# The state space mixer of a two-block model as thirty kinds of step in one fixed order on every engine, without tensor work on GpSimd

## The chip, the cores and the metric

One core of one Trainium2 chip runs the whole program as a single launch. The time is device microseconds (us) of that core. The kernel before took 2540.38 us in the median of three runs (2539.35 to 2540.84); the one execution that the profiler recorded took 2535.84 us.

Engines: PE (TensorE, the matrix engine; PEld is its weight load), DVE (VectorE), ACT (ScalarE), POOL (GpSimd), SP (SyncE, which issues the DMAs here). PE writes its results into PSUM, eight banks of 128x512 float32; DVE and ACT read them from there.

## The reference, cut to what matters

Two blocks of two layers each follow one another on x of 512 positions by 1024 features. Only the first mixer of the first block, a state space mixer, is touched by the change; it stands first in the program.

```python
def s5_mixer(x, a_re, a_im, log_dt, b_re, b_im, c_re, c_im, d_skip, w_glu, w_out):
    u = x.astype(f32).reshape(bsz, seq, SSM_GROUPS, SSM_GROUP)      # 64 groups of 16 features
    dt = jnp.exp(log_dt.astype(f32))[:, None]
    lam_re = jnp.minimum(a_re.astype(f32), -1e-4)
    mag = jnp.exp(lam_re * dt)
    lbar_re = mag * jnp.cos(lam_im * dt)                            # lam_im = a_im
    lbar_im = mag * jnp.sin(lam_im * dt)
...
    bb_re, bb_im = _cmul(coef_re[..., None], coef_im[..., None], b_re, b_im)
    bu_re = jnp.einsum('blgh,gph->lbgp', u, bb_re)
    bu_im = jnp.einsum('blgh,gph->lbgp', u, bb_im)
    _, _, s_re, s_im = lax.associative_scan(                        # s[t] = lbar * s[t-1] + bu[t]
        _ssm_combine, (a_seq_re, a_seq_im, bu_re, bu_im), axis=0)
    y = (jnp.einsum('lbgp,ghp->blgh', s_re, c_re) - jnp.einsum('lbgp,ghp->blgh', s_im, c_im))
    y = y.reshape(bsz, seq, D_MODEL) + d_skip * x
    h = jax.nn.gelu(y).astype(x.dtype)
    val, gate = jnp.split(h @ w_glu, 2, axis=-1)
    z = val * jax.nn.sigmoid(gate)
    return (z @ w_out).astype(x.dtype)
```

After it come a layer norm, a gated feed-forward layer, stick-breaking attention and its feed-forward layer, and then a second block of the same size with other mixers.

## The kernel before, in words

The 64 groups are worked off as eight octets of eight groups. Time is cut into 64 chunks of eight positions, so a group's input is a 128x64 tile (eight positions by sixteen features, by chunks) and an octet's tile is 128x512.

Before the octets, `ssm_params` computes the discretised coefficients for all groups on 128x64 tiles, on DVE, with two sines on ACT (L523, L524), and `ssm_powers` their powers, first for octets 0 and 1 (part 0), later for the others (part 1). An octet then goes through these stages:

- tables (`ssm_tables`, tiles `scr`, `xl`, `xh`): phases on DVE (L605, L609), sine and cosine on ACT;
- matrices (`ssm_mats`): outer products of powers with B and C, 128x1024 each (L625): `m1` and `m2`, summed into `m1` (L634), and `n1` and `n2`, summed into `n1` on POOL (L637). PE multiplies the eight 128x128 blocks of `m1` by `ic` (identity beside C, L648); ACT copies the result out as `bt` and as the `c7` columns (L649, L650); the skip term is added to `c7` on DVE (L655), and after two octets eight DMAs lay `c7` out as the block-triangular `toep`;
- states (`ssm_states`): PE multiplies `bt` by the input (L689); ACT swaps the halves of the result (`sx`), DVE and POOL rotate it by the tables (L701 to L703), DVE scans over chunks with the decay `rho` (L712, a TENSOR_TENSOR_SCAN), rotates it back, and writes `tst` (L714 to L718);
- output (`ssm_out`): PE adds `toep` times input (L733) and `tst` times `n1` (L736), ACT copies to `yo` (L738), PE transposes (L744), ACT applies the GELU (L748), and the result is split into a high part `xh` (ACT, L181) and a low part `xl` (DVE or, for three octets, POOL, L182).

The string `SSM_STEPS` lists the calls of these functions (T, A, B, C). Within what the list gives, a scheduler that works when the program is built orders each engine's instructions. Four blocks of the next layer (`glu`) are used as filling: their weights are loaded and split early (W; `wh` on ACT L174, `wl` on POOL L177), and each finished octet adds its twelve products to four PSUM banks `mm` (G; L196 to L198). The other four banks, `aux`, serve everything else in the mixer. The rest of `glu` follows with banks `acc` and `mm`.

POOL's share is set by `LO_GPSIMD`, `M2_GPSIMD`, `N2_VECTOR` and `DECAY_SCALAR`: by octet, which engine makes `xl`, `m2`, `n2` and the decay row.

Of the kernel before, what the change touches and what calls it, by code (L numbers as in the profile page):

```python
# [39 lines left out]
    "T3 P1 A0 T0 T7 A1 T1 T5 T4 B0 T2 B1 A2 A3 W0 B2 C0 A4 B3 C1 A5 C2 B4 A6 T6 G0 G1 C3 B5 A7 B6 C4 "  # L40
    "G2 B7 G3 C5 C6 C7 G4 G5 G6 G7"
)

LO_GPSIMD, M2_GPSIMD, N2_VECTOR, DECAY_SCALAR = (2, 6, 7), (1,), (0, 1, 3, 5, 6, 7), (0, 2)
# [23 lines left out]

class Kern:
    def __init__(self, tc, ins, out, ctx):  # L70
        self.tc, self.nc, self.i, self.out = tc, tc.nc, ins, out
        self.g = ctx.enter_context(tc.tile_pool(name="glob", bufs=1))
        self.n = 0
        self.ctx = ctx
        self.ph = None
        self.lo_pool = False
        self.nw = 0
        self.nb = 0
        self.boundary = ()
        self.consts()  # L80


    def nm(self, s):
        self.n += 1
        return f"{s}_{self.n}"
# [24 lines left out]
    def scr(self, dt=F32):  # L110
        return self.gt("scr", [P, T], dt, bufs=7)
# [353 lines left out]
    def vexp(self, x, sp):  # L465
# [17 lines left out]
        nc.vector.tensor_add(e, em1, two)  # L483
        t1 = sp()
# [4 lines left out]
    def ssm_params(self):  # L489
# [13 lines left out]
        dt, _ = self.vexp(ldt, sp)  # L503
# [10 lines left out]
        ki, kf, r = sp(I32), sp(), sp()  # L514
# [45 lines left out]
        m2 = sp()  # L560
        V.tensor_mul(m2, mag, mag)
        V.tensor_mul(m2, m2, m2)
        V.tensor_mul(self.rho, m2, m2)

    def ssm_powers(self, part):
# [7 lines left out]
        self.nc.gpsimd.memset(pr[:, 0], 1.0)  # L573
        self.nc.gpsimd.memset(pi[:, 0], 0.0)
# [25 lines left out]
    def ssm_tables(self, o):  # L600

        nc = self.nc
        ph = self.scr()
        v3 = lambda t: t.rearrange("p (g c) -> p g c", c=64)
        nc.vector.tensor_tensor(v3(ph), self.v8[:, 8 * o:8 * o + 8, None].to_broadcast([P, 8, 64]),  # L605
                                self.iota[:, None, :].to_broadcast([P, 8, 64]), op=ALU.mult)
        ki = self.scr()
        nc.scalar.activation(ki, ph, AF.Copy, bias=ROUND)
        nc.vector.scalar_tensor_tensor(ph, ki, ROUND, ph, op0=ALU.subtract, op1=ALU.subtract)  # L609
        s, c = self.gt("xl", [P, T], bufs=NM), self.gt("xh", [P, T], bufs=NM)  # L610
        nc.scalar.activation(s, ph, AF.Sin, scale=TWO_PI)
        nc.scalar.activation(c, ph, AF.Abs)
        nc.scalar.activation(c, c, AF.Sin, scale=-TWO_PI, bias=self.hpi)
        return c, s

    def ssm_mats(self, o, toep, half):
        nc = self.nc
        V = nc.vector
        G8 = slice(8 * o, 8 * o + 8)
        u, bc = self.inp[o]  # L620
        b1, b2, c1, c2 = (bc[:, k * P:(k + 1) * P].rearrange("p (g h) -> p g h", h=16) for k in range(4))

        def outer(eng, tag, bufs, tab, vec):
# [32 lines left out]
        return u, bt, n1  # L656

    def ssm_octet(self, o):

        nc = self.nc  # L660
        if o % 2 == 0:
            self.c7 = self.pt("c7", [P, 2 * P], bufs=2)
        self.half[o] = self.ssm_mats(o, self.c7, o % 2)
        if o % 2 == 0:
            return
        tp = self.toep[o // 2 % len(self.toep)]
        for j in range(8):
            n = 16 * (j + 1)
            nc.sync.dma_start(tp[0:n].rearrange("p (g m) -> p g m", g=16)[:, :, 16 * j:16 * j + 16],
                              self.c7[P - n:P].rearrange("p (g h) -> p g h", g=16))  # L670
        for k in (0, 1):
            self.mats[o - 1 + k] = (tp[:, k * 1024:(k + 1) * 1024], *self.half[o - 1 + k])
# [7 lines left out]
    def ssm_states(self, o):  # L680

        nc = self.nc
        V = nc.vector
        G8 = slice(8 * o, 8 * o + 8)
        tp, u, bt, n1 = self.mats[o]
        co, sn = self.tab[o]
        w = self.aux()
        for g in range(8):
            nc.tensor.matmul(w[:, 64 * g:64 * g + 64], bt[:, g * P:(g + 1) * P], u[:, 64 * g:64 * g + 64],  # L689
                             start=True, stop=True)  # L690

        def swapped(src):

            t = self.pt("sx", bufs=4)
            nc.scalar.activation(t[0:64], src[64:128], AF.Copy)
            nc.scalar.activation(t[64:128], src[0:64], AF.Copy)
            return t

        b = swapped(w)
        a = self.pt("sx", bufs=4)  # L700
        V.tensor_mul(a, co, w)  # L701
        nc.gpsimd.tensor_mul(b, sn, b)
        V.tensor_sub(a, a, b)  # L703
        dec = self.scr()
        d3 = dec.rearrange("p (g c) -> p g c", c=64)
# [47 lines left out]
    def ssm(self):  # L753
# [7 lines left out]
        with ssm_psum as self.ps, self.phase("ssm") as self.ph:  # L761
# [8 lines left out]
            for t in self.toep:  # L770
                nc.gpsimd.memset(t, 0.0)
# [890 lines left out]
```

## Time and profile before

| | |
|---|---|
| median of three runs | 2540.38 us |
| the profiled execution | 2535.84 us |
| its span, first to last instruction | 2534.1 us |
| PE, busy share of the span | 95% |
| DVE | 59% |
| ACT | 39% |
| POOL | 9% |
| last `mm` filling product starts, first `acc` product starts | 181.64, 181.87 us |

The mixer's octets lie in the first 182 us of the span; the program after that is a long run of matrix products. The shares of the table are means over all of it, so the start has to be read from a window of its own. A row of the timeline gives the start, the duration, the engine and line, the operation, output and inputs, shapes, the count of equal instructions in a row, and in brackets the idle time of the engine before it with what ended it. The start of the next row less the start of this one is the pitch at which an engine that doesn't wait works; the duration holds some overlap with the next. One matrix product of float32 operands stands in the trace as two instructions (128 of L648 for 64 in the program).

### The profile page before, as it was taken

The page shows a single profiled execution, that of the slowest core. Times are in us where ns is not written, and L with a number is a line of the kernel's source. Part 1 is how long each engine was busy: PE and PEld are TensorE (multiplying, and loading weights), DVE is VectorE, ACT ScalarE, POOL GpSimd, SP SyncE. Part 2 cuts the span into 40 slices and gives each one's busy share as a digit, 9 for nine tenths or more (in the row PEclk, how much of TensorE's full clock was granted, in tenths as well). Part 3 has the DMA queues.
Part 4 walks back from the last instruction along what each step waited for, and adds up shares of the span by engine and source line. Part 5 has one row for each costly group of instructions (what it writes and reads, how often), then busy time and mean ns, then how long its engine had stood idle before and what let it go on. Part 6 is the DMA issues. An engine that isn't in the chain of part 4 may idle for free. (4 is left out here: it accounts for less than half of the span.)

```text
span 2534.1 us, 30680 instructions
## 1 busy us (share of the span) xinstructions
PE 2404.2 (95%) x12040; PEld 1991.0 (79%) x12044; DVE 1482.7 (59%) x2495; ACT 995.3 (39%) x1541; POOL 219.8 (9%) x158
## 2 busy tenths in 40 slices
PE   1599999999999999999998899999999999999999
PEld 1578888888977778888886678888888887888888
DVE  9963743333677885333458787665435667665622
ACT  2563342222465644222235444333324554333321
POOL 6630100000100010000013201000000000200000
PEclk9799999999999999999999999999999999999999
DMA  3333122233221122222332112222332221223232
GB/s 103 49 62 112 67 100 100 93 93 100 65 92 59 51 67 84 100 100 89 98 97 74 52 42 76 99 92 100 94 98 66 86 84 67 85 99 100 91 111 74
DMA packets 99360, 213.36 MB, mean 84 GB/s; under 512 B 44544, under 2 KB 45184, under 8 KB 99216
## 3 DMA queue, kind: packets, MB, share of 16 engines
q1 hardware_dynamic: 99216, 211.40, 26.3%
q8 instruction: 95, 1.56, 0.3%
q14 instruction: 49, 0.40, 0.0%
HBM read 206.92 MB, written 2.10 MB: 82 GB/s over the span
## 5 line engine op out<-in xcount | busy, mean ns | idle before, releaser
L174 ACT ACTIVATE wh<-wr 128x1024 fp32r<-128x1024 f32 (+1 forms) x389 | 404.5, 1041 | 1011.0 <-PE mm L197 393.1
L177 DVE TENSOR_TENSOR wl<-wr,wh 128x1024 fp32r<-128x1024 f32 (+1 forms) x341 | 408.8, 1199 | 459.5 <-ACT wh L174 458.2
L197 PE MATMUL mm<-xl,wh 128*128 128x512 f32 (+1 forms) x1176 | 453.1, 386 | 0.9 <-DVE xl L182 0.8
L196 PE MATMUL mm<-xh,wh 128*128 128x512 f32 (+1 forms) x1176 | 451.3, 387 | 1.5 <-ACT xh L181 1.3
L198 PE MATMUL mm<-xh,wl 128*128 128x512 f32 (+1 forms) x1176 | 451.7, 385 | 0.0
L197 PE MATMUL acc<-xl,wh 128*128 128x512 f32 (+1 forms) x888 | 336.4, 379 | 6.8 <-DVE xl L182 6.8
L196 PE MATMUL acc<-xh,wh 128*128 128x512 f32 (+1 forms) x888 | 337.2, 380 | 1.2 <-ACT xh L181 1.0
L198 PE MATMUL acc<-xh,wl 128*128 128x512 f32 (+1 forms) x888 | 336.1, 379 | 0.0
L177 POOL TENSOR_TENSOR wl<-wr,wh 128x1024 fp32r<-128x1024 f32 (+1 forms) x48 | 114.6, 2389 | 1890.6 <-ACT wh L174 1825.0
L196 PEld LDWEIGHTS mm<-xh,wh 128*128 128x128 f32 x1176 | 222.4, 190 | 46.0 <-issue 2.9
L197 PEld LDWEIGHTS mm<-xl,wh 128*128 128x128 f32 x1176 | 223.3, 190 | 44.2 <-DVE xl L182 1.7
L198 PEld LDWEIGHTS mm<-xh,wl 128*128 128x128 f32 x1176 | 223.3, 190 | 41.9 <-issue 0.7
L197 PEld LDWEIGHTS acc<-xl,wh 128*128 128x128 f32 x888 | 167.3, 189 | 38.8 <-DVE xl L182 8.1
L196 PEld LDWEIGHTS acc<-xh,wh 128*128 128x128 f32 x888 | 167.5, 189 | 32.9 <-ACT xh L181 1.4
L198 PEld LDWEIGHTS acc<-xh,wl 128*128 128x128 f32 x888 | 167.6, 189 | 30.8
L196 PE MATMUL acc<-hh,wh 128*128 128x512 f32 (+1 forms) x396 | 145.1, 366 | 1.0 <-DVE v L294 1.0
L196 PE MATMUL mm<-hh,wh 128*128 128x512 f32 (+1 forms) x396 | 145.0, 366 | 0.5 <-DVE v L294 0.5
L197 PE MATMUL acc<-hl,wh 128*128 128x512 f32 (+1 forms) x396 | 145.2, 367 | 0.0
L197 PE MATMUL mm<-hl,wh 128*128 128x512 f32 (+1 forms) x396 | 144.8, 366 | 0.0
L198 PE MATMUL mm<-hh,wl 128*128 128x512 f32 (+1 forms) x396 | 144.7, 365 | 0.0
L198 PE MATMUL acc<-hh,wl 128*128 128x512 f32 (+1 forms) x396 | 144.7, 365 | 0.0
L648 PE MATMUL aux<-ic,m 128*128 128x144 f32 x128 | 30.6, 422 | 66.6 <-DVE m L634 62.0
(469 smaller groups left out, 3774.2 us busy)
## 6 DMA issues: line engine op xcount, KB each, us to landing
wr<-down_dram SPq DMA_DIRECT2D x64, 448.0 KB, 3.3
wr<-gu_g_dram SPq DMA_DIRECT2D x44, 512.0 KB, 3.2
wr<-gu_u_dram SPq DMA_DIRECT2D x44, 512.0 KB, 3.2
wr<-gate_dram SPq DMA_DIRECT2D x44, 512.0 KB, 3.2
wr<-up_dram SPq DMA_DIRECT2D x44, 512.0 KB, 3.2
wr<-down_dram SPq DMA_DIRECT2D x32, 512.0 KB, 3.5
wr<-sb_qkv_dram SPq DMA_DIRECT2D x24, 512.0 KB, 3.2
wr<-glu_dram SPq DMA_DIRECT2D x16, 512.0 KB, 3.3
```

Of the source, the lines that this page charges most:

```text
L174: nc.scalar.activation(hi[:, :cols], raw[:, :cols], AF.Copy)
L177: (nc.gpsimd if pool else nc.vector).tensor_sub(lo[:, :cols], raw[:, :cols], hi[:, :cols])
L196: nc.tensor.matmul(ps[:, c0:c1], wh[:, s], xh[k][:, c0:c1], start=st, stop=False)
L197: nc.tensor.matmul(ps[:, c0:c1], wh[:, s], xl[k][:, c0:c1], start=False, stop=False)
L198: nc.tensor.matmul(ps[:, c0:c1], wl[:, s], xh[k][:, c0:c1], start=False, stop=en)
L648: nc.tensor.matmul(p3[:, g - g0], m1[:, g * P:(g + 1) * P], ic[:, g], start=True, stop=True)
```

## The change

Each octet is written as thirty kinds of step (`octet`), and `SSM_STEPS` lists every step of every octet: a letter and the octet's number. The class `InOrder` ties each instruction on DVE, ACT and PE to the one issued before it on that engine, so all three keep the order of the list. The letters: a, b, c, d tables; m, q the outer products `m1`, `m2`; n, N the outer products `n1`, `n2`; i the C columns of `ic`; A, K the matrix products and their copies, in three parts; e, E the skip term and the eight DMAs; B, s, x, y, D, z, t, r, u the states; C, v, X, g, h, l the output and its split; P, Z the powers of part 1 and the phases; W, w, G the filling.

What differs in the work:

- `m1` and `m2` are no longer summed on DVE: PE multiplies both and adds in PSUM. The same holds for `n1` and `n2`, formerly summed on POOL.
- POOL has no tensor work left in the mixer; one 128x8 MEMSET for each octet stays. All sixteen `n1` and `n2`, all `m2`, all first rotations, all `xl` and the filling's `wl` are on DVE; all decay rows, the identity part of `ic` and the clearing of `toep1` are on ACT; the clearing of `toep0` is on DVE.
- The skip term comes laid out from memory (`dd`, 32x1024 instead of 16x64), so POOL's product and its tile go; rows 0 to 63 of the same tile `yd` take the place of `yo`.
- `scr` has nine buffers (seven), `bc` four (two), `n1` and `n2` two each, `tst` four (three).
- The phases and the last two squarings of `rho` move from `ssm_params` to the step Z; an unused part of the first exponential goes.

The diff, cut to its core:

```diff
 SSM_STEPS = (
-    "T3 P1 A0 T0 T7 A1 T1 T5 T4 B0 T2 B1 A2 A3 W0 B2 C0 A4 B3 C1 A5 C2 B4 A6 T6 G0 G1 C3 B5 A7 B6 C4 "
+    "q1 i0 i1 W2 q0 W3 m0 P0 A0 m1 K0 A0 P1 A1 K0 Z0 A0 K1 P2 D1 A1 D0 a1 D2 P3 i2 A1 K1 b1 n0 K1 i3 B1 D3 c1 K0 "
...
-LO_GPSIMD, M2_GPSIMD, N2_VECTOR, DECAY_SCALAR = (2, 6, 7), (1,), (0, 1, 3, 5, 6, 7), (0, 2)
...
+            def call(*args, **kw):
+                self.last = self.kern.after(f(*args, **kw), self.last)
+                for tag in self.kern.fresh:
+                    self.kern.after(self.last, self.kern.taken.get(tag))
+                    self.kern.taken[tag] = self.last
...
-        return self.gt("scr", [P, T], dt, bufs=7)
+        return self.gt("scr", [P, T], dt, bufs=9)
...
-        V.tensor_add(m1, m1, m2)
-        n1 = outer(nc.gpsimd, "n1", 4, pr[:, 1:9], c1)
-        n2 = outer(V if o in N2_VECTOR else nc.gpsimd, "n2", 1, pi[:, 1:9], c2)
-        nc.gpsimd.tensor_add(n1, n1, n2)
...
+                for g in range(g0, g0 + n):
+                    PE.matmul(p3[:, g - g0], L["m1"][:, g * P:(g + 1) * P], ic[:, g], start=True, stop=False)
+                    PE.matmul(p3[:, g - g0], L["m2"][:, g * P:(g + 1) * P], ic[:, g], start=False, stop=True)
...
-        dd = self.pt("dd", [P, P], bufs=1)[96:P]
-        nc.gpsimd.tensor_tensor(gs3(dd, 16), self.dr[96:P, G8, None].to_broadcast([32, 8, 16]),
-                                self.ident[96:P, None, 112:P].to_broadcast([32, 8, 16]), op=ALU.mult)
-        V.tensor_add(toep[96:P, h], toep[96:P, h], dd)
+        def e():
+            V.tensor_add(L["c7"][96:P, half], L["c7"][96:P, half], self.yd[96:P, o * P:(o + 1) * P])
...
-        nc.gpsimd.tensor_mul(b, sn, b)
-        V.tensor_sub(a, a, b)
+        def y():
+            V.tensor_mul(L["b"], L["sn"], L["b"])
+            V.tensor_sub(L["a"], L["a"], L["b"])
...
-        if o in DECAY_SCALAR:
-            nc.scalar.activation(d3, self.rho[:, G8, None].to_broadcast([P, 8, 64]), AF.Copy)
-        else:
-            nc.gpsimd.tensor_copy(d3, self.rho[:, G8, None].to_broadcast([P, 8, 64]))
-        nc.gpsimd.memset(d3[:, :, 0:1], 0.0)
+        def D():
+            L["dec"] = self.scr()
+            A.activation(gc(L["dec"]), self.rho[:, G8, None].to_broadcast([P, 8, 64]), AF.Copy)
+            nc.gpsimd.memset(gc(L["dec"])[:, :, 0:1], 0.0)
...
+                for hf, g in gg:
+                    PE.matmul(yk[hf], L["ts"][:, g, 0:64], L["n1"][:, g * P:(g + 1) * P], start=False, stop=False)
+                for hf, g in gg:
+                    PE.matmul(yk[hf], L["ts"][:, g, 0:64], L["n2"][:, g * P:(g + 1) * P], start=False, stop=True)
...
-        self.split(h, self.xh[o], self.xl[o], nc.gpsimd if o in LO_GPSIMD else nc.vector)
+        def l():
+            self.xl[o] = self.gt("xl", [P, T], F32R, bufs=8)
+            V.tensor_sub(self.xl[o], L["h_"], self.xh[o])
...
-            for t in self.toep:
-                nc.gpsimd.memset(t, 0.0)
-            self.tst = [self.pt(f"tst{k}", [P, 8, 65]) for k in range(3)]
+            nc.vector.memset(self.toep[0], 0.0)
+            nc.scalar.activation(self.toep[1].rearrange("p (n c) -> p n c", c=P),
+                                 self.ident[:, None, :].to_broadcast([P, 16, P]), AF.Copy, scale=0.0)
+            self.tst = [self.pt(f"tst{k}", [P, 8, 65]) for k in range(4)]
...
-                nc.gpsimd.tensor_copy(t[:, :, :P], self.ident[:, None, :].to_broadcast([P, 8, P]))
+                nc.scalar.activation(t[:, :, :P], self.ident[:, None, :].to_broadcast([P, 8, P]), AF.Copy)
...
+                    elif f == "w":
+                        w, raw = fill[o]
+                        self.nc.vector.tensor_sub(w[1], raw, w[0])
```

In the changed kernel every instruction of an octet bears the line of `InOrder`'s call, L84. Three places of the engines' orders follow; the words after the line are the operation, output, inputs and the shape of the output, with x3 for three equal ones.

POOL at the start of the octets, before: the filling's `wl`, the skip product `dd`, the outer products and their sums, a rotation (`sx`).

```order
L177 TENSOR_TENSOR wl_163_597<-wr_161_594,wh_162_596 128x1024
L653 TENSOR_TENSOR dd_96_364<-dr_11_94,ident_1_58 32x128
L177 TENSOR_TENSOR wl_166_603<-wr_164_600,wh_165_602 128x1024
L625 TENSOR_TENSOR n1_90_340<-pw00_18_103,bc_66_259 128x1024
L625 TENSOR_TENSOR n1_107_392<-pw00_18_103,bc_68_263 128x1024
L177 TENSOR_TENSOR wl_169_609<-wr_167_606,wh_168_608 128x1024
L177 TENSOR_TENSOR wl_172_615<-wr_170_612,wh_171_614 128x1024
L625 TENSOR_TENSOR m2_106_389<-pw30_21_106,bc_68_263 128x1024
L637 TENSOR_TENSOR n1_90_340<-n1_90_340,n2_91_342 128x1024
L625 TENSOR_TENSOR n1_145_527<-pw016_22_107,bc_70_267 128x1024
...
L702 TENSOR_TENSOR sx_127_466<-xl_99_372,sx_127_466 128x512
L710 MEMSET scr_129_473 128x8
```

The same engine now, from the clearing of `tst` to the first work after the mixer.

```order
L877 MEMSET tst0_6_84 128x8
L877 MEMSET tst1_7_85 128x8
...
L890 MEMSET pw00_20_104 128x16
...
L775 MEMSET scr_99_370 128x8
L775 MEMSET scr_101_380 128x8
...
L775 MEMSET scr_179_716 128x8
L187 MEMSET mean1_298_1434 128x128
L189 MEMSET ones_299_1436 128x128
L210 TENSOR_TENSOR wl_481_2455<-wr_479_2452,wh_480_2454 128x1024
```

All 1024- and 512-wide tensor work is gone from POOL between the two clearings; what it did stands on DVE, ACT or PE.

ACT at the start, before: the table load, the C columns of `ic`, the two sines of `ssm_params` (`sp`), a filling weight.

```order
L641 ACT_TABLE_LOAD
L641 ACTIVATE ic0_9_90<-bc_66_259 128x8x16
L641 ACTIVATE ic1_10_91<-bc_68_263 128x8x16
L523 ACT_TABLE_LOAD
L523 ACTIVATE sp25_51_186<-sp24_50_179 128x64
L524 ACTIVATE sp26_52_187<-sp24_50_179 128x64
L174 ACTIVATE wh_162_596<-wr_161_594 128x1024
L608 ACTIVATE scr_82_296<-scr_81_294 128x512
```

The same place now.

```order
L84 ACT_TABLE_LOAD
L84 ACTIVATE ic0_10_92<-bc_62_247 128x8x16
L84 ACTIVATE ic1_11_93<-bc_64_252 128x8x16
L873 ACTIVATE toep1_5_81<-ident_1_58 128x2048
L880 ACTIVATE ic0_10_92<-ident_1_58 128x8x128
L880 ACTIVATE ic1_11_93<-ident_1_58 128x8x128
L558 ACT_TABLE_LOAD
L558 ACTIVATE sp23_51_187<-rr_15_99 128x64
L559 ACTIVATE sp24_52_188<-rr_15_99 128x64
...
L84 ACTIVATE bt_91_321<-aux_88_311 128x384
```

The clearing of `toep1` and the identity part of both `ic` stand ahead of the two sines, which read `rr` and whose results `ssm_params` needs.

PE at the start of the octets, before: the matrix products of octets 0 and 1 and the first products with the input.

```order
L648 MATMUL aux_93_347<-ic0_9_90,m1_88_335 128x144 x3
L648 MATMUL aux_94_353<-ic0_9_90,m1_88_335 128x144 x3
L648 MATMUL aux_95_359<-ic0_9_90,m1_88_335 128x144 x2
L648 MATMUL aux_110_399<-ic1_10_91,m1_105_387 128x144 x3
L648 MATMUL aux_111_405<-ic1_10_91,m1_105_387 128x144 x3
L648 MATMUL aux_112_411<-ic1_10_91,m1_105_387 128x144 x2
L689 MATMUL aux_126_457<-v_65_258,bt_92_345 128x64 x8
L689 MATMUL aux_136_494<-v_67_262,bt_109_397 128x64 x8
```

The same place now.

```order
L84 MATMUL aux_88_311<-ic0_10_92,m1_85_299 128x144
L84 MATMUL aux_88_311<-ic0_10_92,m2_81_292 128x144
...
L84 MATMUL aux_92_324<-ic0_10_92,m1_85_299 128x144
L84 MATMUL aux_92_324<-ic0_10_92,m2_81_292 128x144
...
L84 MATMUL aux_93_337<-ic1_11_93,m1_89_318 128x144
L84 MATMUL aux_93_337<-ic1_11_93,m2_77_283 128x144
...
L84 MATMUL aux_97_356<-ic0_10_92,m1_85_299 128x144
L84 MATMUL aux_97_356<-ic0_10_92,m2_81_292 128x144
...
L84 MATMUL aux_104_395<-ic1_11_93,m2_77_283 128x144
L84 MATMUL aux_107_409<-v_63_251,bt_98_361 128x64 x8
L84 MATMUL aux_112_433<-v_61_246,bt_91_321 128x64 x8
```

Each block has two products, one with `m1` and one with `m2`; the parts of octets 0 and 1 are interleaved. Behind the mixer the engines' orders are those of before.

## Rows read from the trace of the kernel before

**Rows 1.** Stretches: length, busy us (instructions) of PE, PEld, DVE, ACT, POOL; clock; DMA
```profile
20.00:60.00 40.00, 7.18 (x28) 6.89 (x29) 39.94 (x72) 12.97 (x25) 25.87 (x10) 1.00 0.16 53
73.00:76.40 3.40, 3.22 (x12) 2.90 (x12) 3.40 (x5) 3.33 (x7) 0.32 (x1) 0.50 0.73 75
60.00:120.00 60.00, 34.26 (x217) 30.70 (x216) 59.75 (x46) 31.51 (x68) 40.03 (x24) 0.73 0.29 47
120.00:160.00 40.00, 36.10 (x260) 31.34 (x260) 35.43 (x35) 25.50 (x46) 23.95 (x18) 0.84 0.27 36
160.00:181.80 21.80, 20.79 (x172) 15.84 (x172) 9.45 (x14) 15.43 (x22) 4.57 (x5) 1.00 0.30 62
```

**Rows 2.** Timeline of PE: start, duration, operation, count
```profile
41.70 4.18 PE L648 MATMUL aux<-ic,m 128*128 128x144 f32 x16 [41.70 <-DVE m L634]
...
73.16 3.22 PE L648 MATMUL aux<-ic,m 128*128 128x144 f32 x12 [7.21 <-DVE m L634]
...
158.40 2.00 PE L689 MATMUL aux<-v,bt 128*128 128x64 f32 x16
...
165.18 0.71 PE L744 MATMUL aux<-ident,yo 64*128 64x64 f32 x8 [0.20 <-ACT yo L738]
...
166.09 0.39 PE L736 MATMUL aux<-n,tst 128*64 128x128 f32 x4
166.31 0.39 PE L733 MATMUL aux<-toep,v 128*64 128x128 f32 x4
...
181.64 0.39 PE L198 MATMUL mm<-xh,wl 128*128 128x512 f32 x1
181.87 0.39 PE L196 MATMUL acc<-xh,wh 128*128 128x512 f32 x1
```

**Rows 3.** Timeline of DVE
```profile
18.31 0.22 DVE L539 TENSOR_TENSOR lb<-sp,sp 128x64 f32<-128x64 f32 x1
18.44 0.22 DVE L540 TENSOR_TENSOR lb<-sp,sp 128x64 f32<-128x64 f32 x1
...
40.34 1.21 DVE L634 TENSOR_TENSOR m<-m,m 128x1024 f32<-128x1024 f32 x1
41.48 0.34 DVE L584 TENSOR_TENSOR pw<-scr,scr 128x192 f32<-128x192 f32 x1
...
44.29 0.68 DVE L605 TENSOR_TENSOR scr<-v,cst 128x512 f32<-128x512 f32 x1
44.89 0.54 DVE L582 TENSOR_TENSOR scr<-pw,coef 128x384 f32<-128x384 f32 x1
...
58.51 3.36 DVE L625 TENSOR_TENSOR m<-pw,bc 128x1024 f32<-128x1024 f32 x1
...
84.05 1.22 DVE L712 TENSOR_TENSOR_SCAN scr<-scr,sx 128x512 f32<-128x512 f32 x1
85.19 0.83 DVE L605 TENSOR_TENSOR scr<-v,cst 128x512 f32<-128x512 f32 x1
...
170.43 0.69 DVE L718 TENSOR_TENSOR tst<-scr,sx 128x512 f32<-128x512 f32 x1
```

**Rows 4.** Timeline of POOL
```profile
58.13 2.66 POOL L637 TENSOR_TENSOR n<-n,n 128x1024 f32<-128x1024 f32 x1 [3.43 <-DVE n L625]
60.87 2.88 POOL L625 TENSOR_TENSOR n<-pw,bc 128x1024 f32<-128x1024 f32 x1
```

**Rows 5.** DVE grouped by line and shape, 0 to 182 us: busy, mean ns
```profile
L625 DVE TENSOR_TENSOR m<-pw,bc 128x1024 f32<-128x1024 f32 x15 | 27.4, 1835 | 0.0
```

**Rows 6.** Timeline of ACT
```profile
8.04 0.31 ACT L641 ACTIVATE ic<-bc 128x128 f32<-128x128 f32 x1 [2.28 <-DMA bc<-bc_dram]
...
13.73 0.26 ACT L523 ACTIVATE sp<-sp 128x64 f32<-128x64 f32 x1 [4.08 <-DVE sp L521]
...
14.04 1.04 ACT L174 ACTIVATE wh<-wr 128x1024 fp32r<-128x1024 f32 x1
...
143.41 1.28 ACT L611 ACT_TABLE_LOAD   x1
```

More of the change, by code (lines that the diff above doesn't have):

```diff
@@ L75, in __init__ @@
         self.ph = None
+        self.fresh, self.taken = [], {}
         self.lo_pool = False
@@ L84, in nm @@
         self.n += 1
+        if isinstance(self.nc, InOrder) and s != "v":
+            self.fresh.append(s)
         return f"{s}_{self.n}"
@@ L483, in vexp @@
         nc.vector.tensor_add(e, em1, two)
+        if not minus1:
+            return e, None
         t1 = sp()
@@ L658, in ssm_octet, with ssm_outer @@
[L658 to L672, printed above, removed]
+    def ssm_outer(self, tag, tab, vec):
+        t = self.pt(tag, [P, 1024], bufs=2)
+        self.nc.vector.tensor_tensor(t.rearrange("p (g j h) -> p g j h", g=8, j=8),
+                                     tab.rearrange("p j g -> p g j")[:, :, :, None].to_broadcast([P, 8, 8, 16]),
+                                     vec[:, :, None, :].to_broadcast([P, 8, 8, 16]), op=ALU.mult)
+        return t
@@ new lines, in C @@
+        @once
+        def C():
+            tp = self.toep[o // 2 % len(self.toep)][:, (o % 2) * 1024:(o % 2 + 1) * 1024]
+            L["y_"] = y = self.aux()
+            for k in range(4):
+                yk = [y[64 * hf:64 * hf + 64, k * P:(k + 1) * P] for hf in (0, 1)]
+                gg = [(hf, 4 * hf + k) for hf in (0, 1)]
+                for hf, g in gg:
+                    PE.matmul(yk[hf], u[:, 64 * g:64 * g + 64], tp[:, g * P:(g + 1) * P], start=True, stop=False)
+                for hf, g in gg:
+                    PE.matmul(yk[hf], L["ts"][:, g, 0:64], L["n1"][:, g * P:(g + 1) * P], start=False, stop=False)
+                for hf, g in gg:
+                    PE.matmul(yk[hf], L["ts"][:, g, 0:64], L["n2"][:, g * P:(g + 1) * P], start=False, stop=True)
@@ new lines, in v, with X @@
+        @once
+        def v():
+            yv = self.yd[0:64].rearrange("c (j g h) -> c g j h", j=8, g=8)
+            for hf in (0, 1):
+                A.activation(yv[:, 4 * hf:4 * hf + 4],
+                             L["y_"][64 * hf:64 * hf + 64].rearrange("c (g j h) -> c g j h", g=4, j=8), AF.Copy)
+            self.v[o] = self.gt("v", [P, T], bufs=NM)
+            nc.sync.dma_start(self.v[o], self.i["xT"][o * P:(o + 1) * P, :])
+        @once
+        def X():
+            L["yt"] = self.aux()
+            for j in range(8):
+                PE.transpose(L["yt"][:, j * 64:(j + 1) * 64], self.yd[0:64, j * P:(j + 1) * P], self.ident[0:64, 0:64])
@@ L753, in ssm @@
+        return S
     def ssm(self):
@@ L799, in ssm @@
             with self.phase("ssmo") as self.ph:
[L800 removed]
+                self.nc, self.taken = InOrder(self), {}
+                steps = [self.octet(o) for o in range(NM)]
+                pw = self.ssm_powers(1)
+                fill, fps, self.c7 = {}, {}, {}
                 for st in SSM_STEPS.split():
                     f, o = st[0], int(st[1])
[L803 to L821 removed]
@@ L822, in ssm @@
+                self.nc = nc
+                self.fresh = []
                 zs = []
```

319 lines of the change are left out of this document (179 added, 140 removed), and 7 rows, old and new, of the table SSM_STEPS.

## The prediction

> **What bounds the kernel now.** I read the busy shares first: PE 95%, DVE 59%. Over the whole span PE is the bound, and nothing behind the mixer changes, so the question is how long the mixer holds PE up. Next the timeline of PE: its first matmul starts at 41.70, having waited for DVE until then, and the first product that belongs to the rest of the program starts at 181.87 [rows 2]. From there on PE has its usual work. A microsecond by which this second point comes earlier is a microsecond of the kernel, as long as the order behind it is the same, which it is.
>
> Then the stretches [rows 1]. From 20 to 120 DVE is busy without a gap (39.94 of 40, 59.75 of 60), PE only 7 and 34 us. From 120 to 160 PE fills up (36.1 of 40), and at the end it is full (20.8 of 21.8). So DVE bounds the first two thirds and PE the last. PE's granted clock follows its load: 0.73 where it was busy for 57% of the time, 0.84 at 90%, 1.00 at 95%.
>
> Last, what keeps DVE busy. The same 128x1024 shape takes 1.21 us at 40.34 and 3.36 at 58.51 [rows 3]. In the second case POOL works from 58.13 to 60.79 and again from 60.87 on [rows 4]; the DVE instruction ends at 61.87. Over the fifteen outer products of L625 into `m` the mean is 1.835 us [rows 5], half more than 1.21. A third of DVE's "busy" time is therefore time in which it is held up beside POOL. This is what the change takes away.
>
> **The change, part by part.** The sums are made against the profiled execution (2535.84, span 2534.1); the median of the runs, 2540.38, is 4.5 above it, and the difference found is taken from the median.
>
> *The start.* Before, the filling's `wl`, clearings and copies on POOL lay beside the small instructions of `ssm_params`, and the first `lb` came at 18.31. Now DVE meets only short clearings there, so the sines decide. ACT has three copies ahead of them: one of 2048 elements (twice the 1.04 of the copy at 14.04) and two of 1024, 4.2 us in all [rows 6]. They start after the second copy of C columns, 8.04 plus 0.31, and with the table load of 1.28 the sines run at 13.8 to 14.3, a little later than the 13.73 of before. The wait that is added is DVE's for the sines, and all that follows on DVE is queued behind it. From there to the first outer product are some 40 small instructions at 0.13 (pitch of 18.31 to 18.44), a few at twice that: 5.5 us, so DVE begins the outer products at 20. PE needs three of them (1.14 each, pitch of 40.34 to 41.48): PE starts at 24 instead of 41.7. The bounds are 22 (exponentials and sines both sooner) and 28 (`lb` at 18.3 as before). Clearing `toep0` on DVE, not shown for this engine, costs 0 to 2.3 (two 1024-wide instructions); it stands ahead of the first load of parameters, which covers it, so I take 0.
>
> *DVE's sum.* From 20 on: 32 outer products and 4 `wl` of 1024 at 1.14 make 41.0; nine 512-wide instructions for each octet, 72 at 0.60 (pitch of 44.29 to 44.89), 43.2; 8 scans at 1.14 (84.05 to 85.19), 9.1; the powers of part 1, phases and skip terms, some 40 instructions, six of them of 384 at 0.54 and the rest between 0.13 and 0.34, 8 to 15, taken as 10. Sum 103. The eight additions of `m1` and `m2` go (9.1), but eleven outer products, eight rotations, three `xl` and four `wl` come over from POOL (12.5 + 4.8 + 1.8 + 4.6): DVE has 15 us more of work of its own than before, but isn't held up in it. Eight 128x8 clearings stay on POOL; their cost to DVE lies between 0 and 8 times 0.34, and I take 0.
>
> *The tail.* From the last `tst` at 170.43 to 181.87 are 11.4 us: output products, copy, transposes, GELU, split, last filling. The last `xl` was on POOL and is now on DVE at 0.6, and the output has one product more; I keep 11. By DVE alone the mixer would then end at 20 + 103 + 11, less 1 for the last `xl` counted twice, which is 133.
>
> *PE's sum, at full clock.* The products with `m1` and `m2` are now 32 trace instructions for each octet, 16 before. Twelve took 3.22 at a clock of 0.50 [rows 1, 2], 0.27 each; no row shows them at full clock, so I take half, 0.134 (an estimate; bounds 0.27, nothing gained, and 0.09, the pace of the eight transposes at 165.18): 256 of them make 34. Products with the input, 2.00 an octet: 16. Output: twelve groups of four at 0.22 (166.09 to 166.31), eight before: 21. Transposes 0.71: 6. Filling: 96 at 0.23 (181.64 to 181.87): 22. Sum 99, of which 24 are new (17 and 7). This is nearly DVE's sum, so PE is the second bound, and the one that the clock stretches.
>
> *The two together.* PE was busy for 90% from 120 to 160 at clock 0.84, and for 95% at 1.00 later. Now it has work all through; I take clock 0.90 and 90%: 99 / 0.90 / 0.90 = 122, from 24 to 146. With 0.84 and 90% it is 155; with 1.00 and 95%, 128, less than DVE allows, so 133. In the 10% lie the new waits of the fixed order. The first: DVE's skip term of octet 1 (e1) stands behind ACT's copies of 32 double products which PE begins cold; behind e1 are queued the phases of octet 3 and the outer products for octets 2 and 3, for which PE waits in turn. DVE gets there at 20 + 16 = 36 (four outer products, the powers, two or three of 512), and PE, at 0.27 for each of 64 trace instructions from 24, at 41 if it stays cold and at 33 if it doesn't: 0 to 5 us, inside the 10%.
>
> *ACT.* From 20 to 181.8 ACT was busy 85 us (13.0 + 31.5 + 25.5 + 15.4, rows 1). It gains six decay rows (at most 1.04 each, taken as 0.6) and two table loads, together 6, and loses nothing: 92 in the 122 us that I give the octets, so it isn't the bound, but each of its copies stands between PE and DVE. A table load is 1.28 in the trace [rows 6], two more are 2.6, and slack covers them. The Trainium skill, "ScalarE: Activation LUTs", section "What ACT_TABLE_LOAD costs", adds a drain of about 1.38 us to each switch. By that the two loads would cost 5.3, and by the row 2.6; in neither case does ACT's sum reach PE's.
>
> *DMAs and buffers.* SP's order puts the eight transfers of octets 2 and 3 for `toep` behind two inputs that wait for PE's output products. What waits for them is the output of octet 2, which comes after. The first two filling weights no longer wait for POOL. More buffers only remove waits. I take 0; the bound is one late transfer, some 3 us.
>
> So the mixer ends at 146 instead of 182, and the difference is 36: 2540 - 36 = 2504.
>
> **The rivals.**
>
> *A, DVE alone.* PE stays at full clock and hides all waits: end at 133, 49 less, 2491. For it: clock 1.00 at 95% load. Against: PE has never been that full before 160, and the first octets are a chain.
>
> *B, POOL isn't the cause.* DVE's long instructions come from something else that stays (PE's and ACT's use of PSUM, DMAs). Then 103 becomes 103 x 1835 / 1210 = 156, end at 20 + 156 + 10 = 186, and the kernel is at 2544, or 2530 if the excess stays in half of it. For it: the rows only show a coincidence in time. Against: late, with POOL idle for most of 160 to 181.8, the same kinds take their short times (0.69 at 170.43).
>
> *C, PE at the clock of 60 to 120.* With 0.73 and 90% busy the end is at 24 + 151 = 175: 2533. With fewer waits (0.73, 100%) it is 160: 2518. For it: 73 to 76.4, where after a wait of 7.21 PE worked at 0.50 with 95% load [rows 1, 2]. Against: that was behind DVE, which now is quicker.
>
> *D, slower: PE falls to half clock and stays there.* Its place is the doubled products: the fixed order interleaves short parts of two octets with copies by ACT, and every part waits for a bank. If each wait takes the clock back, 99 becomes 198, end at 222, 40 more: 2580. It decides from a mean clock of 99 / 158 = 0.63 downwards at full load, below any long stretch of before after 60.
> The Trainium skill, "TensorE: Matmul & The Clock Gate", section "HAM oscillation — how this bites in real kernels", says that bursts of matmuls between waits lose the full clock again each time, and that a kernel that does so stays far below its peak. By that rule the time goes to D's if the parts of the doubled products are waited for one by one. The trace agrees in part (0.50 after the wait of 7.21, 1.00 at 95% load).
>
> **How the numbers follow.** Forecast, end between 136 and 156 (2494 to 2514): 0.64. A: 0.11. C: 0.14. B: 0.06. D: 0.05. About 0.2%, 5 us, is what a measurement of this kernel can tell from no change. Faster by more than that: forecast, A and nearly all of C, 0.89. Within it: most of B and a little of C, 0.06. Slower: D and the rest of B, 0.05. The range reaches from A's 2490 to 2528, the middle of C; outside are the far half of C, B, D and a corner of A, some 0.18.
>
> **What would show it.** In the changed profile: the first PE matmul near 24; DVE's 1024-wide instructions all at 1.2 and none above 2; DVE with idle stretches that end on ACT or PE; the mixer's PE clock at 0.85 to 0.95 and PE busy for 90% from 30 on; the first `acc` product near 146, and after it the same length as before, 2352 us. Wrong would be: long DVE instructions with POOL idle (B); PE busy but at 0.5 to 0.7 (C, D); a start above 28; or a rest of the program that isn't as long as it was.

## The result, and the profile after

| | before | changed |
|---|---|---|
| median (runs) | 2539.98 us (4) | 2511.88 us (4; 2507.85 to 2512.5) |
| the profiled execution, its span | 2535.84, 2534.1 | 2507.85, 2506.1 |
| first PE matmul | 41.70 | 24.33 |
| first `acc` product: the mixer's end | 181.87 | 150.88 |
| from there to the end | 2352.2 | 2355.2 |

The ratio is 0.9886 (95%: 0.9869 to 0.9903), 28.1 us less; the profiled executions differ by 28.0 as well. The mixer ends 31.0 us earlier, and 3.0 are lost behind it.

Stretches of the changed kernel (length, busy us of PE, PEld, DVE, ACT, POOL, clock, DMA), to be set against [rows 1]; the last is PE's whole share of the mixer:

```profile
20.00:60.00 40.00, 30.17 (x228) 29.12 (x228) 36.19 (x67) 18.64 (x46) 0.45 (x4) 0.91 0.24 42
60.00:120.00 60.00, 49.49 (x443) 45.38 (x440) 54.16 (x69) 49.21 (x91) 0.45 (x4) 0.89 0.38 77
24.33:150.88 126.55, 109.23 (x929) 99.29 (x930) 104.73 (x155) 89.79 (x167) 1.25 (x10) 0.92 0.32 61
```

PE's busy time from 20 to 60 has gone from 7 to 30, and its clock from 60 to 120 from 0.73 to 0.89. DVE is no longer busy throughout: 36 of 40, 54 of 60.

The clock column has to be read with care where PE begins:

```profile
24.33:29.60 5.27, 5.27 (x22) 5.27 (x23) 4.89 (x22) 0.59 (x2) 0.00 (x0) 1.00 0.00 0
29.60:34.80 5.20, 5.20 (x44) 5.20 (x43) 4.99 (x13) 3.70 (x11) 0.34 (x3) 1.00 0.00 0
```

The granted clock is 1.00 in both rows, yet the first 5.27 us hold half as many products as the next 5.20. PE works at half pace there, as it does before at 41.70 (4.18 for 16, also with 1.00 beside it in [rows 1]).

PE's timeline after, for [rows 2]:

```profile
24.33 10.64 PE L84 MATMUL aux<-ic,m 128*128 128x144 f32 x64 [24.33 <-DVE pw L84]
...
68.66 2.29 PE L84 MATMUL aux<-ic,m 128*128 128x144 f32 x8 [5.90 <-DVE sx L84]
...
101.96 5.61 PE L84 MATMUL aux<-ic,m 128*128 128x144 f32 x44
...
150.65 0.39 PE L84 MATMUL mm<-xh,wl 128*128 128x512 f32 x1
150.88 0.39 PE L229 MATMUL acc<-xh,wh 128*128 128x512 f32 x1
```

At 101.96, at full clock, a product of the matrices takes 5.61 / 44 = 0.128. At 68.66 PE has waited 5.90, its longest wait after the start.

DVE after, for [rows 3]: the start, and the wait that holds PE up at 68.66.

```profile
13.59 0.22 DVE L566 TENSOR_TENSOR lb<-sp,sp 128x64 f32<-128x64 f32 x1 [1.88 <-ACT sp L558]
...
20.69 3.50 DVE L84 TENSOR_TENSOR m<-pw,bc 128x1024 f32<-128x1024 f32 x3
...
60.52 1.22 DVE L84 TENSOR_TENSOR wl<-wr,wh 128x1024 fp32r<-128x1024 f32 x1 [1.89 <-ACT wh L84]
...
67.92 0.69 DVE L84 TENSOR_TENSOR sx<-xh,aux 128x512 f32<-128x512 f32 x1 [2.32 <-ACT xh L84]
```

Both late waits end on ACT. ACT's timeline (the brackets name what it waited for) shows why: it waits for the raw filling weights W1 and W0, and the tables `xh` stand behind them in its list.

```profile
59.43 1.06 ACT L84 ACTIVATE wh<-wr 128x1024 fp32r<-128x1024 f32 x1 [3.13 <-DMA wr<-glu_dram]
...
65.04 1.06 ACT L84 ACTIVATE wh<-wr 128x1024 fp32r<-128x1024 f32 x1 [2.52 <-DMA wr<-glu_dram]
66.00 0.61 ACT L84 ACTIVATE xl<-scr 128x512 f32<-128x512 f32 x1
66.52 0.61 ACT L84 ACTIVATE xh<-scr 128x512 f32<-128x512 f32 x1
```

DVE by shape, 0 to 200 us after, for [rows 5] (busy, mean ns, idle before):

```profile
L84 DVE TENSOR_TENSOR m<-pw,bc 128x1024 f32<-128x1024 f32 x16 | 19.1, 1217 | 0.1
L84 DVE TENSOR_TENSOR_SCAN scr<-scr,sx 128x512 f32<-128x512 f32 x8 | 9.7, 1218 | 0.1
L84 DVE TENSOR_TENSOR sx<-xh,aux 128x512 f32<-128x512 f32 x8 | 5.4, 679 | 5.1 <-ACT xh L84 3.0 <-ACT sx L84 2.0
L84 DVE TENSOR_TENSOR sx<-sx,sx 128x512 f32<-128x512 f32 x8 | 5.5, 692 | 0.3
```

The last three in the kernel before:

```profile
L703 DVE TENSOR_TENSOR sx<-sx,sx 128x512 f32<-128x512 f32 x8 | 10.6, 1324 | 3.0 <-POOL sx L702 2.9
L712 DVE TENSOR_TENSOR_SCAN scr<-scr,sx 128x512 f32<-128x512 f32 x8 | 9.8, 1222 | 0.2
L701 DVE TENSOR_TENSOR sx<-xh,aux 128x512 f32<-128x512 f32 x8 | 5.4, 678 | 0.5 <-ACT sx L696 0.5
```

The outer products fall from 1.835 to 1.217, the subtractions into `sx` from 1.324 to 0.692. The scan and the product that reads `aux` from PSUM took the same before as after.

The 3.0 us behind the mixer lie in one place. The same part of the second block, after and then before (up to there the changed kernel is 30.7 ahead):

```profile
1425.60:1432.40 6.80, 6.80 (x20) 3.46 (x20) 3.53 (x10) 2.63 (x5) 0.00 (x0) 0.50 0.05 19
```

```profile
1456.30:1463.10 6.80, 6.80 (x35) 4.49 (x34) 5.35 (x17) 3.08 (x6) 0.00 (x0) 1.00 0.05 17
```

The clock is at 0.50 there after, and PE does fewer instructions in the same time: 6.8 us at half clock cost up to 3.4. Of the runs below, whose order behind the mixer is the same, e5 falls to 0.50 there by the trace's record of the clock and e6 doesn't, so it isn't that order that decides it.

### The profile page after: what moved, and what is told of

Its sections match the earlier page's. It is cut to its first block, busy times and chain, and to the rows that moved or that the text cites. A ratio compares the mean times of both kernels' runs of the same rounds, so it can differ in the third digit from the quotient of the medians.

```text
span 2506.1 us, 31148 instructions
## 1 busy us (share of the span) xinstructions
PE 2417.5 (96%) x12296; PEld 2006.6 (80%) x12300; DVE 1445.8 (58%) x2512; ACT 1004.9 (40%) x1552; POOL 117.9 (5%) x106
## 5 line engine op out<-in xcount | busy, mean ns | idle before, releaser
L230 PE MATMUL mm<-xl,wh 128*128 128x512 f32 (+1 forms) x1144 | 439.9, 385 | 0.0
L229 PE MATMUL mm<-xh,wh 128*128 128x512 f32 (+1 forms) x1144 | 439.2, 387 | 0.2 <-ACT scr L1309 0.2
L231 PE MATMUL mm<-xh,wl 128*128 128x512 f32 (+1 forms) x1144 | 438.4, 384 | 0.0
L229 PEld LDWEIGHTS mm<-xh,wh 128*128 128x128 f32 x1144 | 216.5, 190 | 42.7 <-issue 2.8
L230 PEld LDWEIGHTS mm<-xl,wh 128*128 128x128 f32 x1144 | 217.3, 190 | 40.9 <-issue 0.7
L231 PEld LDWEIGHTS mm<-xh,wl 128*128 128x128 f32 x1144 | 217.2, 190 | 40.6 <-issue 0.4
L210 POOL TENSOR_TENSOR wl<-wr,wh 128x1024 fp32r<-128x1024 f32 (+1 forms) x44 | 105.1, 2391 | 1901.6 <-ACT wh L207 1839.4
L229 PEld LDWEIGHTS acc<-hh,wh 128*128 128x128 f32 x396 | 74.6, 188 | 13.5 <-DVE v L327 1.4
```

Of the source, the lines that this page charges most:

```text
L210: (nc.gpsimd if pool else nc.vector).tensor_sub(lo[:, :cols], raw[:, :cols], hi[:, :cols])
L229: nc.tensor.matmul(ps[:, c0:c1], wh[:, s], xh[k][:, c0:c1], start=st, stop=False)
L230: nc.tensor.matmul(ps[:, c0:c1], wh[:, s], xl[k][:, c0:c1], start=False, stop=False)
L231: nc.tensor.matmul(ps[:, c0:c1], wl[:, s], xh[k][:, c0:c1], start=False, stop=en)
```

## The experiments

My theory: beside POOL's work DVE's instructions take longer, and what it holds up holds PE up. Rivals: the fixed order, the buffers or the double products bring the gain. First all results; "mixer" is the first `acc` product in the profile, "rest" what follows it in that one execution. Each ratio is to the kernel before as it was run beside that experiment (medians from 2537.72 to 2540.75), so compare experiments by the mixer and the ratio, not by the medians.

| run | first matmul | mixer | rest | median | ratio to before (95%) |
|---|---|---|---|---|---|
| before | 41.70 | 181.87 | 2352.2 | 2539.98 | |
| e1 before, POOL idle | 29.07 | 162.56 | 2351.2 | 2520.46 | 0.9919 (0.9904 to 0.9934) |
| e9 e1, double products | 26.11 | 169.58 | 2355.5 | 2526.76 | 0.9952 (0.9939 to 0.9966) |
| e3 changed, single products | 25.41 | 162.58 | 2353.7 | 2519.42 | 0.9924 (0.9907 to 0.9941) |
| changed | 24.33 | 150.88 | 2355.2 | 2511.88 | 0.9886 (0.9869 to 0.9903) |
| e2 changed, idle POOL work | 59.54 | 198.55 | 2354.7 | 2554.82 | 1.0065 (1.0048 to 1.0083) |
| e4 changed, scheduler's order | 21.74 | 140.71 | 2353.9 | 2497.89 | 0.9842 (0.9825 to 0.9858) |
| e5 third raw buffer | 24.09 | 147.02 | 2353.7 | 2503.31 | 0.9867 (0.9849 to 0.9884) |
| e6 ACT free | 23.82 | 147.13 | 2354.0 | 2505.89 | 0.9871 (0.9855 to 0.9886) |
| e7 DVE free | 22.14 | 150.55 | 2355.0 | 2508.61 | 0.9885 (0.9868 to 0.9901) |
| e8 PE free | 24.18 | 149.74 | 2354.5 | 2506.42 | 0.9875 (0.9860 to 0.9890) |
| e10 e4, third raw buffer | 21.93 | 139.95 | 2353.2 | 2496.37 | 0.9832 (0.9818 to 0.9845) |
| e11 e10, `toep1` cleared on DVE | 22.28 | 140.77 | 2353.7 | 2496.28 | 0.9829 (0.9815 to 0.9842) |
| e12 e5, list edited | 23.28 | 144.47 | 2359.9 | 2503.81 | 0.9852 (0.9835 to 0.9869) |

**e1: POOL's work alone.**

```diff
-LO_GPSIMD, M2_GPSIMD, N2_VECTOR, DECAY_SCALAR = (2, 6, 7), (1,), (0, 1, 3, 5, 6, 7), (0, 2)
+LO_GPSIMD, M2_GPSIMD, N2_VECTOR, DECAY_SCALAR = (), (), range(8), range(8)
-        n1 = outer(nc.gpsimd, "n1", 4, pr[:, 1:9], c1)
+        n1 = outer(V, "n1", 4, pr[:, 1:9], c1)
-        nc.gpsimd.tensor_add(n1, n1, n2)
+        V.tensor_add(n1, n1, n2)
-        nc.gpsimd.tensor_mul(b, sn, b)
+        V.tensor_mul(b, sn, b)
...
```

> The kernel before with POOL's octet work (n1, its sum, n2, m2, rotation, xl, wl, skip product) on DVE and the decay rows on ACT; order by the scheduler, single products on PE, old buffers. POOL theory: with POOL idle the 1024-wide instructions of DVE fall from a mean of 1.8 to 1.2; DVE has 121 us of work (103 and sixteen more additions at 1.14) from about 22 on, so with 5 to 10% of waits the first acc product starts at 155 to 165 instead of 181.9, and the kernel takes 2514 to 2524. Rival, POOL isn't the cause: the long instructions stay, DVE gets some 33 us of work more at half again the time, the mixer ends at 215 or later, 2570 or more. Rival, the fixed order is the cause: without it nothing is gained, 2535 or more.

The mixer ends at 162.56, 19.3 earlier, though DVE has more to do. The outer products by shape:

```profile
L625 DVE TENSOR_TENSOR m<-pw,bc 128x1024 f32<-128x1024 f32 x16 | 19.4, 1220 | 0.0
```

As the theory had it. Taking the work off POOL is worth about two thirds of the mixer's 31.

**e2: POOL's work put back, with no one waiting for it.**

```diff
             L["m1"] = self.ssm_outer("m1", rev(self.powers(o)[2]), b1)
+            for _ in range(4):
+                nc.gpsimd.tensor_tensor(self.idle, self.idle, self.idle, op=ALU.mult)
...
```

> The changed kernel with 32 multiplications of 128x896 on POOL that read and write a tile nobody else uses (some 2.1 us each, 67 in all). POOL theory: DVE instructions beside them grow from 1.2 to between 2.4 and 3.4, DVE loses half or more of the 67 us where they lie in the mixer, the first acc product comes 15 to 35 us later than 150.9, 2527 to 2547. Rival, POOL isn't the cause: DVE's durations stay at 1.2 and the time at 2508 to 2514.

POOL's timeline, then DVE's in the same stretch:

```profile
3.23 43.88 POOL L696 TENSOR_TENSOR idle<-idle 128x896 f32<-128x896 f32 x25
```

```profile
24.35 1.72 DVE L515 TENSOR_TENSOR sp<-sp,sp 128x64 f32<-128x64 f32 x1
26.11 1.72 DVE L516 TENSOR_TENSOR sp<-sp,sp 128x64 f32<-128x64 f32 x1
...
48.01 0.23 DVE L515 TENSOR_TENSOR sp<-sp,sp 128x64 f32<-128x64 f32 x1
...
75.96 2.69 DVE L84 TENSOR_TENSOR n<-pw,bc 128x1024 f32<-128x1024 f32 x1
```

While POOL works, a DVE instruction of 64 elements can take 1.72 instead of 0.23, about as long as one of POOL's (43.88 / 25 = 1.76): it waits for a whole instruction, however short it is itself. Not each one waits: in the timeline about every second one does, and the next takes some 0.2 (0.21 at 29.51). Later an outer product beside POOL takes 2.69 instead of 1.22. The direction was right and my price too low: three quarters of POOL's work fell into the small instructions of the start, its 56 us (32 at a mean of 1.754) cost 47.7, and the first matmul came 35.2 later.

**e3: the sums back on DVE.**

```diff
+        def summed(p, q):
+            if p in L and q in L:
+                V.tensor_add(L[p], L[p], L[q])
...
-                    PE.matmul(p3[:, g - g0], L["m2"][:, g * P:(g + 1) * P], ic[:, g], start=False, stop=True)
```

> The changed kernel with m1 + m2 and n1 + n2 summed on DVE again and single products on PE. If DVE bounds the first two thirds: sixteen additions at 1.14 are 18 us more on DVE, PE's 24 us less are of no use, the first acc product comes 5 to 18 us later than 150.9, 2517 to 2530. Rival, PE and its clock bound: PE is done 5 to 10 us earlier, 2502 to 2507.

11.7 later, as expected if DVE bounds. Beside it stands something I had not expected, in the stretch of 60 to 120:

```profile
60.00:120.00 60.00, 38.65 (x291) 34.27 (x291) 55.37 (x69) 42.83 (x83) 0.45 (x4) 0.67 0.34 72
```

With less work on PE, and more on the engine that it waits for, PE's clock is 0.67 instead of 0.89. Over the mixer PE is busy for 99 us instead of 109, so of the 24 us that the forecast's prices give for the second products only 10 are saved.

e3 also ends its mixer where e1 does (162.58 and 162.56): in the fixed order, the finer list and the buffers gain nothing without the double products.

**e4: the same steps without the tie.**

```diff
-                self.nc, self.taken = InOrder(self), {}
+                self.taken = {}
```

> The changed kernel without the tie that holds each engine to the order of the list; the scheduler orders the same steps. If the work moved is what counts: the mixer ends at 155 to 165, 2515 to 2525. If the fixed order is what counts: the gain is gone, 2535 or more. If the fixed order costs more in waits than it brings: below 2507.

The third of the cases: the mixer ends at 140.71, 10.2 before the fixed order, and PE waits 3.92 at most after its start.

```profile
21.74 2.63 PE L722 MATMUL aux<-ic,m 128*128 128x144 f32 x8 [21.74 <-DVE m L642]
...
58.53 0.85 PE L722 MATMUL aux<-ic,m 128*128 128x144 f32 x2 [3.92 <-ACT c L734]
...
140.71 0.39 PE L229 MATMUL acc<-xh,wh 128*128 128x512 f32 x1
```

**e5: a third raw buffer, order kept.**

```diff
...
-                        raw, w = self.wt("wr", F32, 2), [self.wt(n, F32R, 4) for n in ("wh", "wl")]
+                        raw = self.pt("w1r", (P, 1024)) if o == 1 else self.wt("wr", F32, 2)
+                        w = [self.wt(n, F32R, 4) for n in ("wh", "wl")]
```

> The changed kernel, fixed order kept, with a third buffer for the raw filling weights (the phase's value is worked out in place to make room), so that the loads of the two late weights needn't wait for the low parts of the first two. If ACT's waits for these loads (3.13 and 2.52 us at 59 and 65 us), behind which its copies for DVE and PE are queued, are what the fixed order costs: the first acc product starts 4 to 6 us before 150.9, 2505 to 2508. Rival, the cost is spread over many small waits: within 2 us of 150.9, 2510 to 2514.

3.9 earlier, just short of my 4 to 6. Neither of ACT's two late weights waits any longer (W1, from the new buffer, then W0):

```profile
56.66 1.04 ACT L84 ACTIVATE wh<-w1r 128x1024 fp32r<-128x1024 f32 x1
...
59.80 1.06 ACT L84 ACTIVATE wh<-wr 128x1024 fp32r<-128x1024 f32 x1
```

**e6 to e8: one engine freed.** In `InOrder`, for e6:

```diff
-        self.vector, self.scalar, self.tensor = (self.Engine(kern, e) for e in (nc.vector, nc.scalar, nc.tensor))
+        self.vector, self.scalar, self.tensor = self.Engine(kern, nc.vector), nc.scalar, self.Engine(kern, nc.tensor)
```

> The changed kernel with only ACT free of the fixed order (DVE and PE tied). If ACT's place in the list costs the 10 us between the fixed order (150.9) and the scheduler's (140.7): first acc product at 141 to 145, 2498 to 2504. If another engine's does: 149 to 152, 2509 to 2514.

> The changed kernel with only DVE free. If the waits of DVE's queue (for wh, for the tables, for the C copies; 9 us between 49 and 86) are what costs: first acc product at 141 to 145, 2498 to 2504. If ACT's order costs, DVE gains only the start, some 2.6 us: 147 to 150, 2506 to 2511.

> The changed kernel with only PE free. If it is PE's order (matrix products of later octets queued behind products that wait for the scan or the transfers to toep; waits of 17 us in all after 24.3): first acc product at 141 to 146, 2499 to 2506. If PE only waits for what DVE and ACT have not done yet: 149 to 152, 2509 to 2514.

ACT free is worth 3.7, about as much as the third raw buffer, and between my two cases. PE free is worth 1.1, in the second case by the mixer. DVE free is worth 0.3, less than either case: PE begins 2.2 earlier, but that doesn't reach the mixer's end. The three single gains sum to 5.2 of the 10.2 that come when all are free (e4). That an engine which moves ahead then meets another that doesn't would explain it; it isn't shown, and no run freed two engines.

**e9: double products in the old kernel, POOL idle.**

```diff
-        V.tensor_add(m1, m1, m2)
...
+                nc.tensor.matmul(p3[:, g - g0], m2[:, g * P:(g + 1) * P], ic[:, g], start=False, stop=True)
```

> Run e1 (the kernel before, no octet work on POOL, scheduler's order, old buffers) with the sums of m1, m2 and n1, n2 taken from DVE and made by double products on PE, as in the changed kernel. If taking sixteen additions from DVE and keeping PE fuller is worth the same here as between e3 and the changed kernel (11.7 us): first acc product at 149 to 154 instead of 162.6, 2506 to 2512. If PE then stays at half clock: 160 or later, 2517 or more.

A miss: 7.0 later than e1. The time lies in the second case, but its reason doesn't hold: PE's clock over the mixer is 0.88, and 0.82 in e1. DVE's waits in e9:

```profile
75.11 1.23 DVE L625 TENSOR_TENSOR m<-pw,bc 128x1024 f32<-128x1024 f32 x1 [1.82 <-DMA bc<-bc_dram]
...
102.64 0.29 DVE L654 TENSOR_TENSOR c<-c,dd 32x128 f32<-32x128 f32 x1 [4.38 <-ACT c L649]
...
137.67 0.69 DVE L713 TENSOR_TENSOR scr<-xh,scr 128x512 f32<-128x512 f32 x1 [3.93 <-ACT sx L695]
```

DVE is busy for 104 us instead of e1's 119 and waits for ACT's copies and for the two `bc` buffers. The edit also leaves `n1` two buffers instead of four; outer products `n` wait for PE's output products four times, 2.4 us in all. So in the old kernel the double products cost 7.0, and beside the finer list and the new buffers they gain 11.7 (e3). How list and buffers share this wasn't tried.

**e10, e11: the best versions.** The edit of e5 in e4; and the clearing of `toep1`:

```diff
-            nc.scalar.activation(self.toep[1].rearrange("p (n c) -> p n c", c=P),
-                                 self.ident[:, None, :].to_broadcast([P, 16, P]), AF.Copy, scale=0.0)
+            nc.vector.memset(self.toep[1], 0.0)
```

> The changed kernel in the scheduler's order (as e4) with the third raw buffer of e5. If the loads still hold ACT there (0.57 us at 59, a product waiting 3.9 us at 58.5): first acc product at 137 to 139.5 instead of 140.7, 2494 to 2496. If the scheduler has already found other work for these waits: 140 to 141.5, 2496 to 2499.

> As e10, with toep1 cleared on DVE at the start instead of by a copy of 1.89 us on ACT ahead of the sines. If the sines hold DVE (1.01 us before the first lb): everything comes 1 us earlier than in e10. If the second clearing, 1.76 us on DVE ahead of the parameters, delays DVE instead: 0 to 2 us later than e10.

0.8 earlier, between my two cases, and then 0.8 later: the scheduler has already found other work for most of these waits, and the clearing gains nothing. e4, e10 and e11 can't be told apart in time; all beat both kernels.

**e12: the list edited by hand.**

```diff
-    "q1 i0 i1 W2 q0 W3 m0 P0 A0 m1 ...
+    "i0 i1 W2 q0 W3 m0 q1 P0 A0 m1 ...
...
-    ... K2 i4 e2 N1 B2 K3 m4 A3 s2 q4 c3 "
+    ... K2 i4 N1 B2 K3 m4 A3 e2 s2 q4 c3 "
...
```

> Run e5 (fixed order, third raw buffer) with two moves in the list: q1, the outer product of octet 1, from the first place to behind m0, so that PE's first products come one outer product (1.14) sooner; and e2, the skip term for which DVE waited 2.30 us on ACT's C copies, from before N1 to behind m4, past two outer products. If these two waits lie on the path: first acc product 2 to 3.4 us before e5's 147.0, so 143.6 to 145, 2499.9 to 2501.3 against e5's median of 2503.3. If other waits of the fixed order take their place: within 1 us of 147.0, 2502 to 2504.5.

The mixer ends at 144.47, 2.6 earlier, as expected. The time can't confirm it: the ratios to the kernel before, 0.9852 and 0.9867, differ by some 3.8 us the expected way, but their intervals overlap, and the medians (2503.81 and 2503.31) were not taken side by side. In the profiled execution, e12's slowest, the rest is 6.2 longer than in e5's, for instance here; then e5 in the same place:

```profile
1960.70:1967.50 6.80, 6.80 (x23) 5.29 (x22) 2.70 (x8) 2.10 (x6) 0.00 (x0) 0.50 0.00 0
```

```profile
1960.05:1966.85 6.80, 6.80 (x36) 5.49 (x35) 3.08 (x10) 1.99 (x6) 0.00 (x0) 1.00 0.00 0
```

By the trace's record of the clock, the rest of e12 has 45 us at 0.50 and that of e5 31; half of the difference is 7, near the 6.2.

## Why the prediction was right, and what it missed

The forecast was 2504, the median is 2511.88. Of the 8 us between them 4.9 lie in the mixer and 3.0 behind it.

*The start* was right: outer products from 20.69 (forecast 20), first matmul at 24.33 (24), with DVE's added wait for the sines. Two errors partly cancel in it: DVE went on at 13.59, some 0.9 sooner than forecast, and the small instructions then took 7.1 instead of 5.5.

*DVE's sum* was right. The 1024-wide instructions take 1.2 throughout. The mixer's DVE instructions from 20.69 on are 107 us of busy time; I had 103. The mechanism, POOL, is shown by e1 and e2. That one of the two waits for the other's whole instruction is also seen the other way round, in POOL's timeline of the kernel before, where the small product `dd` takes 0.60 alone and 1.31 when it begins beside the scan that starts at 84.05 [rows 3], and again beside three later scans:

```profile
54.10 0.60 POOL L653 TENSOR_TENSOR dd<-dr,ident 32x128 f32<-32x128 f32 x1
...
84.16 1.31 POOL L653 TENSOR_TENSOR dd<-dr,ident 32x128 f32<-32x128 f32 x1 [0.30 <-DVE c L655]
```

So the scan's unchanged time doesn't mean that it met nothing: it came first and held POOL up. The Trainium skill, "SBUF — State Buffer", section "Who interferes with whom", says that a DVE instruction with two inputs in SBUF and a GpSimd one that reads SBUF share a port, and that the later one blocks until the first has ended. The traces agree: 1.72 for an instruction of 0.23, and no change where one input lies in PSUM (means of 0.678 before and 0.679 after, and 0.67 at 76.94 before, in the middle of a product on POOL).

*PE's sum* was right: 109.23 busy at a mean clock of 0.92 is 100 at full clock, or 98 when the first 5.27 us, recorded at 1.00, count as half; I had 99, and 0.134 for the product that took 0.128.

*ACT's sum* was right: 90 busy (forecast 92). The two added table loads cost their 1.28 and nothing beside it: the one at 115.47 begins as the copy before it ends (114.83 plus 0.63), and the next activation starts at 116.77.

*The two together* is the step that was short. I took 90% busy at 0.90, 122 us; it was 86% (109.23 of 126.55) at 0.92. PE waits 17 instead of 12, and the mixer ends at 150.9 instead of 146. The 0.90 came out near, but the rule I took it from, that the clock follows PE's load, isn't in the rows: 20 to 60 has 1.00 at 18% load and 73 to 76.4 has 0.50 at 95% [rows 1]. That the value fitted is partly luck. Most of the 4.9 comes from the term "DMAs and buffers 0": the fixed order loads W1 and W0 only after DVE has freed a raw buffer, and ACT, then DVE, then PE wait for it. e5 gives it back: 3.9 of the 4.9. My bound had been one late transfer, some 3 us, and I left it out of the sum. Of the 10.2 that the fixed order costs, this is 3.9, and the two moves of e12 give back another 2.6; the rest isn't located. The wait I did name, DVE at e1, did not occur: ACT's copies were done in time.

*The same length afterwards* failed by 3.0: not by another order but by a stretch at half clock. Other executions differ there by more, so this says nothing of the change.

Rival B falls with e1 and e2. (Its 2530 for half the excess doesn't follow from its own sum: 20 + 130 + 10 is 160, or 2518.) A, C and D did not come: the clock was 0.92 over the mixer. What D needs, a wait before each part of the doubled products, did not arise: the 64 of octets 0 and 1 ran on from 24.33 without one. A mean clock near D's 0.63 is found in e3 (0.67 from 60 to 120), where PE had less to do.

What I had not asked is whether the fixed order helps at all. With the same steps it costs 10.2 us of the mixer (e4). The mixer's 31.0 are thus 19.3 for POOL's work (e1) and 21.9 for double products, finer list and buffers under the scheduler's order (e1 to e4), less the 10.2. What part each of the last three has stays open (e3, e9).

## What to carry to other kernels

Before work is moved to POOL as a spare engine, look at DVE's time for one shape beside it and without: here 56 us of POOL cost 48 (e2). An order that is fixed on all engines turned two late transfers into a wait of the whole chain here (e5), so try the same steps under the scheduler, and look for the wait that three engines share. Judge a change of a few microseconds by a point in the trace behind which the order is the same, not by the time alone.

## What the runs showed of the hardware that I had not expected

- With work taken from PE and given to the engine that PE waits for, the clock fell as well: in e3 from 0.89 to 0.67 between 60 and 120. How much of the 11.7 us lost is due to the clock isn't separated.
- The granted clock can stand at 1.00 while PE works at half pace: 22 product instructions in the first 5.27 us of the changed kernel's octets, 44 in the next 5.20.
- Two executions with the same instructions in the rest of the program differ by up to 8.7 us there (2351.2 in e1, 2359.9 in e12), with 27 and 45 us at half clock.
- A DVE instruction of 0.23 took as long as the POOL instruction that it met, 1.72 (e2). Most of that run's loss, 35.2 of 47.7 us, came at the start, where DVE's instructions are small.
